# A row maximum on one core: 20 loads instead of 22, narrower parts for GpSimd, another ending

## The chip, the cores and the metric

The kernel runs on 1 core of one Trainium2 chip. The metric is the device time in microseconds (us) of one execution. Times are compared between fast runs only: one of the first runs of the kernel before took 183.46 us, over 1.5% above the others, counts as slow and is left out of every ratio.

## The reference

The input is 32 x 512 x 1024 float32 (67.1 MB), the output the maximum over the last axis (64 KB).

```python
def reference(x: np.ndarray) -> np.ndarray:      # x: (32, 512, 1024) float32
    return np.max(x, axis=-1).astype(np.float32)
```

The 16,384 rows of 1024 are 128 on each of the 128 partitions. In this text "row" means one row on each partition, 512 KiB.

## The kernel before

The loads go into a ring of 46 rows. Each is reduced by one instruction of the vector engine (DVE). Load sizes in rows, numbered from 0, get smaller so that little is left to do when the last has landed:

```python
BLOCKS = [
    [15, 15, 15, 13, 13, 11, 9, 9, 6, 6],
    [3, 3, 2, 1, 1, 1, 1, 1, 1, 1],
]
RING = 46
BY_GPSIMD = {8: 1, 9: 3, 12: 1}      # whole rows of these loads
MERGE = {9: 8, 15: 9, 18: 12}        # after which load DVE takes the result
```

Five whole rows go by another road: TensorE transposes eight parts of 128 x 128 into PSUM, the memory that it writes (`turn`), ScalarE copies them to SBUF, where the ring lies, GpSimd takes the maximum across partitions, TensorE transposes it back (`back`), and DVE merges the eight partial maxima of each row.

```python
    for c in range(C):                                   # turn; C is 8
        in_turn("PE", nc.tensor.transpose(out=ps[:, c * P:(c + 1) * P],
            in_=rows[:, k, c * P:(c + 1) * P], identity=ident))
    nc.scalar.copy(out=sb, in_=ps)
    nc.gpsimd.partition_all_reduce(top, sb, P, bass_isa.ReduceOp.max)
    # ... cut: back, the loop over the loads
```

The last row comes in two halves; the second reduce takes the first one's result along as an extra column. The first 112 columns of results are stored once the last whole-row load is reduced, the last 16 at the end, both from ScalarE's queue.

```python
    in_turn("DVE", nc.vector.reduce_max(out=tail[:, PAD - 1:PAD], in_=half, axis=X))
    in_turn("DVE", nc.vector.reduce_max(out=res[:, I - 1:], in_=tail[:, PAD - 1:], axis=X))
    store = nc.scalar.dma_start(out=views[0][0], in_=views[0][1])
    tc.add_manual_dep(store.ins, reduce.ins.name, SYNC, reason="behind the loads")
    nc.scalar.dma_start(out=views[1][0], in_=views[1][1])
```

## Time and profile before

| what | kernel before |
|---|---|
| median of the first three runs | 164.4 us |
| span of the profiled run | 162.6 us |
| DVE busy | 135.0 us, 83% |
| GpSimd (POOL) busy | 16.3 us, 10% |
| load queue, share of the 16 DMA engines' time | 96.6% |
| DVE waiting for loads | 24.3 us, of which 18.9 for the first |

A profile has several views. The page gives busy shares and groups of equal instructions. The timeline gives start, length and, in brackets, the idle time ahead of an instruction with what ended it. The chain is the sequence of work and waits that led to the end. One thing to know of the timeline: it brackets waits of some size only. Waits below about 0.15 us must be read from the distance between starts. The lines of before are in the prediction below.

The groups show what one instruction costs. The columns are line, engine, operation, shapes, count, then busy time and mean length in ns, then idle time ahead:

```profile
L139 DVE TENSOR_REDUCE res<-ring 128x1 f32<-128x1024 f32 x8 | 9.4, 1212 | 0.0
L106 POOL PARTITION_ALL_REDUCE top<-sb x5 | 16.1, 3255 | 138.8 <-ACT sb L104 138.8
L143 DVE TENSOR_REDUCE res<-fetched 128x1 f32<-128x8 f32 x2 | 0.3, 154 | 0.0
```

A row costs DVE 1.2 us by itself, a merge 0.15 us, and a row costs GpSimd 3.3 us.

### The profile page before, as it was taken

The page shows a single profiled execution, that of the slowest core. Times are in us where ns is not written, and L with a number is a line of the kernel's source. Part 1 is how long each engine was busy: PE and PEld are TensorE (multiplying, and loading weights), DVE is VectorE, ACT ScalarE, POOL GpSimd, SP SyncE. Part 2 cuts the span into 40 slices and gives each one's busy share as a digit, 9 for nine tenths or more (in the row PEclk, how much of TensorE's full clock was granted, in tenths as well). Part 3 has the DMA queues.
Part 4 walks back from the last instruction along what each step waited for, and adds up shares of the span by engine and source line. Part 5 has one row for each costly group of instructions (what it writes and reads, how often), then busy time and mean ns, then how long its engine had stood idle before and what let it go on. Part 6 is the DMA issues. An engine that isn't in the chain of part 4 may idle for free.

```text
span 162.6 us, 293 instructions
## 1 busy us (share of the span) xinstructions
PE 13.0 (8%) x80; PEld 11.7 (7%) x80; DVE 135.0 (83%) x33; ACT 6.3 (4%) x6; POOL 16.3 (10%) x9
## 2 busy tenths in 40 slices
PE   0000000000000000000000000000000040943520
PEld 0000000000000000000000000000000030933420
DVE  3000079995999779999996999999999999999994
ACT  3000000000000000000000000000000011240200
POOL 0000000000000000000000000000000007099910
PEclk9999999999999999999999999999999999985555
DMA  7999699988999799999998989999999999999990
GB/s 242 484 484 438 287 484 484 484 378 348 484 484 484 333 498 432 445 419 419 419 419 387 499 388 427 417 426 408 417 435 435 471 399 426 423 418 409 406 368 16
DMA packets 3456, 67.18 MB, mean 413 GB/s; under 512 B 640, under 2 KB 640, under 8 KB 1792
## 3 DMA queue, kind: packets, MB, share of 16 engines
q1 hardware_dynamic: 3168, 67.11, 96.6%
q10 hardware_dynamic: 288, 0.07, 0.2%
HBM read 67.11 MB, written 0.07 MB: 413 GB/s over the span
## 4 chain that ended last, share of the span: by engine, by line
DVE 54%; DMA 44%; SPq 0%; issue 0%
DVE res L139 53%; DMA ring<-in_x_dram 44%; DVE res L156 0%; DVE tail L155 0%; SPq L133 0%; DVE res L143 0%
## 5 line engine op out<-in xcount | busy, mean ns | idle before, releaser
L139 DVE TENSOR_REDUCE res<-ring 128x1 f32<-128x1024 f32 (+6 forms) x20 | 132.1, 6653 | 24.3 <-DMA ring<-in_x_dram 24.3
L106 POOL PARTITION_ALL_REDUCE top<-sb x5 | 16.1, 3255 | 138.8 <-ACT sb L104 138.8
L98 PE MATMUL ps<-ident,ring 128*128 128x128 f32 x40 | 8.1, 382 | 134.2 <-DMA ring<-in_x_dram 131.8
L98 PEld LDWEIGHTS ps<-ident,ring 128*128 128x128 f32 x40 | 7.1, 204 | 134.3 <-issue 134.2
L104 ACT COPY sb<-ps 128x1024 f32<-128x1024 f32 x5 | 5.1, 1013 | 144.9 <-PE ps L98 143.0
L115 PE MATMUL fetched<-ident,top 1*128 1x1 f32 x40 | 5.0, 243 | 9.1 <-POOL top L106 9.1
L115 PEld LDWEIGHTS fetched<-ident,top 1*128 1x128 f32 x40 | 4.6, 214 | 10.3 <-POOL top L106 9.8
L104 ACT ACT_TABLE_LOAD x1 | 1.3, 1283 | 0.7 <-PEq L176 0.7
L76 DVE MEMSET ident<- 128x128 f32 x1 | 0.2, 165 | 0.8 <-PEq L176 0.8
L156 DVE TENSOR_REDUCE res<-tail 128x1 f32<-128x513 f32 x1 | 0.7, 686 | 0.0
L155 DVE TENSOR_REDUCE tail<-ring 128x1 f32<-128x512 f32 x1 | 0.7, 675 | 0.0
L83 DVE TENSOR_SCALAR rowno<-rowno 32x1 f32<-32x1 f32 x3 | 0.4, 147 | 0.1
L143 DVE TENSOR_REDUCE res<-fetched 128x1 f32<-128x8 f32 (+1 forms) x3 | 0.5, 161 | 0.0
L78 DVE TENSOR_TENSOR_SCAN colno<-ident 128x128 f32<-128x128 f32 x1 | 0.4, 425 | 0.0
L85 DVE TENSOR_SCALAR ident<-colno,rowno 128x128 f32<-128x128 f32 x1 | 0.3, 287 | 0.0
L80 DVE STREAM_TRANSPOSE rowno<-colno 128x32 f32<-128x32 f32 x1 | 0.2, 211 | 0.0
L176 POOL MEMSET const-float32-0.0<- 128x1 f32 x1 | 0.1, 99 | 0.2 <-issue 0.2
L176 POOL MEMSET const-uint8-127<- 128x1 uint8 x1 | 0.1, 103 | 0.0
L176 POOL MEMSET const-bfloat16-1.0<- 128x1 bf16 x1 | 0.1, 102 | 0.0
L176 POOL MEMSET const-float32-1.0<- 128x1 f32 x1 | 0.1, 99 | 0.0
L77 DVE MEMSET rowno<- 128x32 f32 x1 | 0.1, 85 | 0.0
## 6 DMA issues: line engine op xcount, KB each, us to landing
ring<-in_x_dram SPq DMA_DIRECT2D x3, 7680.0 KB, 38.4
ring<-in_x_dram SPq DMA_DIRECT2D x2, 6656.0 KB, 34.6
ring<-in_x_dram SPq DMA_DIRECT2D x2, 4608.0 KB, 37.8
ring<-in_x_dram SPq DMA_DIRECT2D x2, 3072.0 KB, 31.9
ring<-in_x_dram SPq DMA_DIRECT2D x1, 5632.0 KB, 28.6
ring<-in_x_dram SPq DMA_DIRECT2D x7, 512.0 KB, 22.3
ring<-in_x_dram SPq DMA_DIRECT2D x2, 1536.0 KB, 34.9
ring<-in_x_dram SPq DMA_DIRECT2D x1, 1024.0 KB, 33.4
```

Of the source, the lines that this page charges most:

```text
L78: in_turn("DVE", nc.vector.tensor_tensor_scan(out=colno, data0=ident, data1=ident, initial=-1.0, op0=ALU.add, op1=ALU.mult))
L83: in_turn("DVE", nc.vector.tensor_scalar(out=part, in0=part, scalar1=float(q * 32), scalar2=None, op0=ALU.add))
L85: in_turn("DVE", nc.vector.tensor_scalar(out=ident, in0=colno, scalar1=rowno[:, 0:1], scalar2=None, op0=ALU.is_equal))
L98: in_turn("PE", nc.tensor.transpose(out=ps[:, c * P:(c + 1) * P], in_=rows[:, k, c * P:(c + 1) * P], identity=ident,))
L104: nc.scalar.copy(out=sb, in_=ps)
L106: nc.gpsimd.partition_all_reduce(top, sb, P, bass_isa.ReduceOp.max)
L115: in_turn("PE", nc.tensor.transpose(out=backs[j][:, k, c:c + 1], in_=tops[j, k][0:1, c * P:(c + 1) * P], identity=ident[0:1, 0:1],))
L139: reduce = in_turn("DVE", nc.vector.reduce_max(out=cols[:, :n - m], in_=xc[:, :n - m, :], axis=X))
L143: in_turn("DVE", nc.vector.reduce_max(out=tiles[i][1], in_=backs[i], axis=X))
L155: in_turn("DVE", nc.vector.reduce_max(out=tail[:, PAD - 1:PAD], in_=half, axis=X))
L156: in_turn("DVE", nc.vector.reduce_max(out=res[:, I - 1:], in_=tail[:, PAD - 1:], axis=X))
L176: nc = _bacc.Bacc("TRN2", target_bir_lowering=False, num_devices=1)
```

## The change

It aims at the last 70 us, where DVE runs without a break behind the loads: other load sizes, GpSimd's share cut into parts 128 wide and spread over five loads, the last two rows in three pieces, and the first store in three parts by partitions.

```diff
-    [15, 15, 15, 13, 13, 11, 9, 9, 6, 6],
-    [3, 3, 2, 1, 1, 1, 1, 1, 1, 1],
+    [15, 15, 15, 14, 12, 11, 9, 8, 7, 6],
+    [4, 3, 2, 2, 1, 1, 1],
-BY_GPSIMD = {8: 1, 9: 3, 12: 1}
-MERGE = {9: 8, 15: 9, 18: 12}
+SHARED = {7: (2, 3), 9: (4, 4), 11: (3, 3), 13: (2, 3), 16: (1, 1)}   # load: (rows, parts of each)
+MERGE = {8: (7,), 12: (9,), 15: (11,), 18: (13, 16)}
 ... (order of TensorE's work, loads issued up to three ahead: cut)
+    if m and parts < C:                    # the rest of shared rows, to PSUM
+        maximum(share(j)[:, parts, :], rows(j)[:, n - m:, parts * P:])
-    in_turn("DVE", nc.vector.reduce_max(out=tail[:, PAD - 1:PAD], in_=half, axis=X))
-    in_turn("DVE", nc.vector.reduce_max(out=res[:, I - 1:], in_=tail[:, PAD - 1:], axis=X))
+    nc.sync.dma_start(out=piece, in_=xb[:, S - 2, :D - K])                  # 689 columns
+    nc.sync.dma_start(out=res[:, AT:AT + K + W], in_=pair[:, D - K:D + W])  # 671
+    nc.sync.dma_start(out=res[:, MID:], in_=pair[:, D + W:])                # 688
+    latest_row = maximum(res[:, AT - 1:AT], piece)
 ... (one reduce for both halves of the pair, merges, the last reduce: cut)
-    store = nc.scalar.dma_start(out=views[0][0], in_=views[0][1])
+    for p, q in ((0, 48), (48, 96), (96, P)):
+        store = nc.scalar.dma_start(out=views[0][0][p:q], in_=views[0][1][p:q])
```

More of the change, by code (lines that the diff above doesn't have):

```diff
@@ L13 @@
 BLOCKS = [
-    [15, 15, 15, 13, 13, 11, 9, 9, 6, 6],
-    [3, 3, 2, 1, 1, 1, 1, 1, 1, 1],
+    [15, 15, 15, 14, 12, 11, 9, 8, 7, 6],
+    [4, 3, 2, 2, 1, 1, 1],
 ]
 RING = 46
-TENSOR = {
-    8: [("turn", 8, 0), ("back", 8, 0)],
-    9: [("turn", 9, 0), ("turn", 9, 1), ("turn", 9, 2), ("back", 9, 0)],
-    12: [("turn", 12, 0), ("back", 9, 1), ("back", 9, 2), ("back", 12, 0)],
-}
-BY_GPSIMD = {8: 1, 9: 3, 12: 1}
-MERGE = {9: 8, 15: 9, 18: 12}
+SHARED = {7: (2, 3), 9: (4, 4), 11: (3, 3), 13: (2, 3), 16: (1, 1)}
+TENSOR = [
+    ("turn", 7, 0), ("back", 7, 0), ("turn", 9, 0), ("turn", 9, 1),
+    ("back", 9, 0), ("turn", 11, 0), ("turn", 11, 1), ("back", 9, 1),
+    ("turn", 13, 0), ("back", 11, 0), ("back", 11, 1), ("turn", 16, 0),
+    ("back", 13, 0), ("back", 16, 0),
+]
+MERGE = {8: (7,), 12: (9,), 15: (11,), 18: (13, 16)}
 NOSYNC = mybir.DependencyInfo(mybir.DependencyClass.NoSync, mybir.DependencyReason.DATA)
@@ L53 @@
     allr = ctx.enter_context(tc.tile_pool(name="allr", bufs=2))
-    psum = ctx.enter_context(tc.tile_pool(name="psum", bufs=3, space=bass.MemoryType.PSUM))
-    psmall = ctx.enter_context(tc.tile_pool(name="psmall", bufs=2, space=bass.MemoryType.PSUM))
+    psum = ctx.enter_context(tc.tile_pool(name="psum", bufs=2, space=bass.MemoryType.PSUM))
+    psmall = ctx.enter_context(tc.tile_pool(name="psmall", bufs=4, space=bass.MemoryType.PSUM))
     ring = once.tile([P, RING, D], F32)
-    res = once.tile([P, I], F32)
-    PAD = 16
-    tail = once.tile([P, PAD + H], F32)
+    W = 336
+    K = W - 1
+    AT = I + 16
+    MID = AT + K + W + 17
+    res = once.tile([P, MID + D - W], F32)
     latest = {}
@@ L86 @@
         out=ident, in0=colno, scalar1=rowno[:, 0:1], scalar2=None, op0=ALU.is_equal))
-    tiles = {}
-    tops = {}
-    backs = {}
-    def turn(j, k):
-        rows, cols = tiles[j]
-        ps = psum.tile([P, D], F32)
-        for c in range(C):
-            in_turn("PE", nc.tensor.transpose(
-                out=ps[:, c * P:(c + 1) * P],
-                in_=rows[:, k, c * P:(c + 1) * P],
-                identity=ident,
-            ))
-        sb = turned.tile([P, D], F32)
-        nc.scalar.copy(out=sb, in_=ps)
-        top = allr.tile([P, D], F32)
-        nc.gpsimd.partition_all_reduce(top, sb, P, bass_isa.ReduceOp.max)
-        tops[j, k] = top
-    def back(j, k):
-        if j not in backs:
-            fetched = psmall.tile([P, BY_GPSIMD[j], C], F32)
-            backs[j] = fetched
-        for c in range(C):
-            in_turn("PE", nc.tensor.transpose(
-                out=backs[j][:, k, c:c + 1],
-                in_=tops[j, k][0:1, c * P:(c + 1) * P],
-                identity=ident[0:1, 0:1],
-            ))
-    at = first = j = 0
+    loads = []
+    first = at = 0
     views = []
-    for loads in BLOCKS:
-        S = sum(loads) + (loads is BLOCKS[-1])
+    for sizes in BLOCKS:
+        S = sum(sizes) + 2 * (sizes is BLOCKS[-1])
         xb = xf[first * P:(first + S) * P, :].rearrange("(p i) d -> p i d", p=P)
@@ L128 @@
         b = 0
-        for n in loads:
+        for n in sizes:
             if at + n > RING:
                 at = 0
-            xc = ring[:, at:at + n, :]
-            nc.sync.dma_start(out=xc, in_=xb[:, b:b + n, :])
-            cols = res[:, first + b:first + b + n]
-            m = BY_GPSIMD.get(j, 0)
-            tiles[j] = xc[:, n - m:, :], cols[:, n - m:]
-            for what, i, k in TENSOR.get(j, []):
-                (turn if what == "turn" else back)(i, k)
-            reduce = in_turn("DVE", nc.vector.reduce_max(
-                out=cols[:, :n - m], in_=xc[:, :n - m, :], axis=X))
-            if j in MERGE:
-                i = MERGE[j]
-                in_turn("DVE", nc.vector.reduce_max(out=tiles[i][1], in_=backs[i], axis=X))
+            loads.append((at, n, xb[:, b:b + n, :], first + b))
@@ L144, with chunks, rows, turn @@
             at += n
             b += n
-            j += 1
         first += S
     assert first == I
+    def chunks(j):
+        m, parts = SHARED[j]
+        per = max(1, C // parts)
+        return [(r, min(per, m - r)) for r in range(0, m, per)]
+    def rows(j):
+        start, n, _, _ = loads[j]
+        return ring[:, start:start + n, :]
+    tops = {}
+    backs = {}
+    def turn(j, c):
+        m, parts = SHARED[j]
+        r, q = chunks(j)[c]
+        W = q * parts * P
+        ps = psum.tile([P, D], F32)
+        for i in range(q):
+            for c0 in range(parts):
+                k = i * parts + c0
+                in_turn("PE", nc.tensor.transpose(
+                    out=ps[:, k * P:(k + 1) * P],
+                    in_=rows(j)[:, loads[j][1] - m + r + i, c0 * P:(c0 + 1) * P],
+                    identity=ident,
+                ))
+        sb = turned.tile([P, D], F32)
+        in_turn("ACT", nc.scalar.copy(out=sb[:, :W], in_=ps[:, :W]))
+        top = allr.tile([P, D], F32)
+        in_turn("POOL", nc.gpsimd.partition_all_reduce(
+            top[:, :W], sb[:, :W], P, bass_isa.ReduceOp.max))
+        tops[j, c] = top
@@ new lines, in share, with back @@
+    def share(j):
+        m, parts = SHARED[j]
+        if j not in backs:
+            fetched = psmall.tile([P, parts + (parts < C), m], F32)
+            backs[j] = fetched
+        return backs[j]
+    def back(j, c):
+        m, parts = SHARED[j]
+        r, q = chunks(j)[c]
+        for i in range(q):
+            for c0 in range(parts):
+                k = i * parts + c0
+                in_turn("PE", nc.tensor.transpose(
+                    out=share(j)[:, c0, r + i:r + i + 1],
+                    in_=tops[j, c][0:1, k * P:(k + 1) * P],
+                    identity=ident[0:1, 0:1],
+                ))
@@ new lines, in maximum, with merge @@
+    def maximum(out, in_):
+        return in_turn("DVE", nc.vector.reduce_max(out=out, in_=in_, axis=X))
+    def merge(j):
+        for i in MERGE.get(j, ()):
+            _, k, _, c0 = loads[i]
+            q, _ = SHARED[i]
+            maximum(res[:, c0 + k - q:c0 + k], share(i).rearrange("p k m -> p m k"))
+    issued = done = 0
+    todo = list(TENSOR)
+    for j in range(len(loads)):
+        while issued < len(loads) and issued < j + 3:
+            start, n, src, _ = loads[issued]
+            held = any(s < start + n and start < s + k for s, k, _, _ in loads[j:issued])
+            if held:
+                break
+            nc.sync.dma_start(out=rows(issued), in_=src)
+            issued += 1
+        while todo and todo[0][1] < (j if todo[0][0] == "back" else issued):
+            what, i, c = todo.pop(0)
+            (turn if what == "turn" else back)(i, c)
+        _, n, _, col = loads[j]
+        m, parts = SHARED.get(j, (0, 0))
+        if n > m:
+            maximum(res[:, col:col + n - m], rows(j)[:, :n - m, :])
+        if m and parts < C:
+            maximum(share(j)[:, parts, :], rows(j)[:, n - m:, parts * P:])
+        merge(j)
@@ L150 @@
+    for what, i, c in todo:
+        assert what == "back"
+        back(i, c)
     if at + 1 > RING:
         at = 0
-    half = ring[:, at, :H]
-    nc.sync.dma_start(out=half, in_=xb[:, b, :H])
-    nc.sync.dma_start(out=tail[:, PAD:], in_=xb[:, b, H:])
-    in_turn("DVE", nc.vector.reduce_max(out=tail[:, PAD - 1:PAD], in_=half, axis=X))
-    in_turn("DVE", nc.vector.reduce_max(out=res[:, I - 1:], in_=tail[:, PAD - 1:], axis=X))
-    store = nc.scalar.dma_start(out=views[0][0], in_=views[0][1])
@@ L160 @@
-    tc.add_manual_dep(store.ins, reduce.ins.name, SYNC, reason="behind the loads")
+    piece = ring[:, at, :D - K]
+    nc.sync.dma_start(out=piece, in_=xb[:, S - 2, :D - K])
+    pair = xb[:, S - 2:, :].rearrange("p i d -> p (i d)")
+    nc.sync.dma_start(out=res[:, AT:AT + K + W], in_=pair[:, D - K:D + W])
+    nc.sync.dma_start(out=res[:, MID:], in_=pair[:, D + W:])
+    latest_row = maximum(res[:, AT - 1:AT], piece)
+    merge(len(loads))
+    maximum(
+        bass.AP(tensor=res.tensor, offset=res.offset + I - 2,
+                ap=[list(res.ap[0]), [MID - 1 - (I - 2), 2]]),
+        res[:, AT - 1:AT + K + W].rearrange("p (r k) -> p r k", r=2))
@@ L161 @@
+    merge(len(loads) + 1)
+    maximum(res[:, I - 1:I], res[:, MID - 1:])
+    for p, q in ((0, 48), (48, 96), (96, P)):
+        store = nc.scalar.dma_start(out=views[0][0][p:q], in_=views[0][1][p:q])
+        tc.add_manual_dep(store.ins, latest_row.ins.name, SYNC, reason="behind the loads")
     nc.scalar.dma_start(out=views[1][0], in_=views[1][1])
```

## The prediction

> **What bounds the kernel now.** I read the page first: busy shares, then the chain that ended last, then the groups by shape, then the timeline of the vector engine (DVE) and of the load queue (SPq). The page's first lines:
>
> ```profile
> span 162.6 us, 293 instructions
> PE 13.0 (8%) x80; PEld 11.7 (7%) x80; DVE 135.0 (83%) x33; ACT 6.3 (4%) x6; POOL 16.3 (10%) x9
> q1 hardware_dynamic: 3168, 67.11, 96.6%
> DVE 54%; DMA 44%; SPq 0%; issue 0%
> ```
>
> Loads keep the DMA engines busy for 96.6% of the span and DVE is busy for 83%, so the two are nearly balanced. The chain shows how they share the path. In order of time (start, length, what):
>
> ```profile
> 1.15 38.43 DMA ring<-in_x_dram
> ...
> 39.60 16.16 DVE res L139
> ...
> 55.78 33.41 DMA ring<-in_x_dram
> ...
> 89.22 53.79 DVE res L139 x6
> ...
> 159.05 0.60 DVE tail L155
> ...
> 159.67 0.69 DVE res L156
> ```
>
> Until 89.22 us the chain passes through transfers; from there it is DVE without a break, to 160.36. So what counts is how long DVE waits before it becomes the bound, and how much work it has after that. The waits stand in the timeline (start, busy, then in brackets the idle time before):
>
> ```profile
> 39.60 16.15 DVE L139 TENSOR_REDUCE res<-ring 128x15 f32<-128x15360 f32 x1 [1.99 <-DMA ring<-in_x_dram]
> 57.75 30.08 DVE L139 TENSOR_REDUCE res<-ring 128x15 f32<-128x15360 f32 x2 [1.99 <-DMA ring<-in_x_dram]
> 89.22 53.79 DVE L139 TENSOR_REDUCE res<-ring 128x13 f32<-128x13312 f32 x6 [1.40 <-DMA ring<-in_x_dram]
> ```
>
> A start after a wait is also the time at which a load landed. More landings are to be had from the load queue: it has at most 8 loads in flight, so late loads issue when the one 8 places before has landed. The queue's timeline has issues at
>
> ```profile
> 131.68 0.33 SPq L133 DMA_DIRECT2D ring<-in_x_dram  x1
> 138.98 0.33 SPq L133 DMA_DIRECT2D ring<-in_x_dram  x1
> 146.35 0.33 SPq L133 DMA_DIRECT2D ring<-in_x_dram  x1
> 150.13 0.33 SPq L154 DMA_DIRECT2D tail<-in_x_dram  x1
> ```
>
> and the last (the tail) lands 9.0 us after issue by the page's table of DMA issues, at 159.13.
>
> **A model of the loads.** Below, "row" is one row of 1024 per partition, 512 KiB. A load of n rows takes a*n + c of a saturated queue. The third load of 15 rows lands 57.75 - 39.60 = 18.15 us after the second, so 15a + c = 18.15. From 57.73 to the tail at 159.13 there are 83 rows in 19 loads: 83a + 19c = 101.40. This gives a = 1.2047 us a row, c = 0.074 us a load. Check: load 8, counting from 0, has 61 rows and 6 loads after 57.73, so 131.66; the queue shows 131.68.
>
> **What the Trainium skill says.** "DMA: Bandwidth & Descriptors", section Bandwidth, puts the fabric ceiling at 435 GB/s. Here 524,288 bytes in 1.2047 us are 435 GB/s: it agrees, the queue has nothing to give but c. The section Rules for kernel authors of the same page says of two transfers to disjoint partition halves not to bother, as both use all 16 engines; no run yet shows this for a store. "VectorE: DVE Perf Modes", the perf-mode tier table, gives tensor_reduce only the 1x mode. It agrees: one row is 1024/0.96 GHz = 1.067 us, and the group of 1-row reduces has a mean of 1212 ns, the 15-row one 16153 ns, both columns/0.96 plus 0.15. The section on the TRN2 errata there says that a fixed part is exposed between instructions. Here back-to-back reduces start columns/0.96 plus 0.065 to 0.09 us apart (53.71 us from 89.22 to the first merge for 51,200 columns in 6 reduces; 11.13 us for 10,240 in the next 6). I use 0.08. No page gives the width dependence of the GpSimd all-reduce.
>
> **The change, part by part.** The loads change from 15,15,15,13,13,11,9,9,6,6 and 3,3,2,1x7,.5,.5 to 15,15,15,14,12,11,9,8,7,6 and 4,3,2,2,1,1,1 and three pieces of two thirds of a row.
>
> *Idle time of DVE.* Load 3 now lands at 57.73 + 14a + c = 74.67. DVE is done with load 2 at 57.75 + 16.15 = 73.90, and starts 0.03 after landing, at 74.70: a wait of 0.80. Load 4 lands at 89.20 as before, and DVE finishes load 3 at 74.70 + 14.93 + 0.07 = 89.70, so the wait of 1.40 is gone. **Saving: 0.60 us.**
>
> *Work of DVE.* GpSimd had 1 + 3 + 1 whole rows, 40 parts of 128 columns. It gets 2x3 + 4x4 + 3x3 + 2x3 + 1x1 = 38. So it takes less, not more; DVE gets 256 columns, **0.27 us**. After load 2, DVE has 24 instructions from load 3 on against 22 before (the order of instructions shows five added reduces of the rest of shared rows, which write to PSUM, and one more merge; there are fewer load reduces): 2 x 0.08 = **0.16 us**. Net: -0.60 + 0.27 + 0.16 = **-0.17 us**.
>
> The same as a sum: from 74.70, 69 whole rows (70,656 columns), the rests of shared rows (1280 + 2048 + 1920 + 1280 + 896 = 7,424), merges (52) and the pieces (689 + 672 + 689) are 80,182 columns, 83.52 us; 23 gaps of 0.08 are 1.84, and the end of the last one 0.15. DVE ends at 160.21, against 160.36. The same sum for before, 66,601 columns from 89.22, gives 69.38 + 21 x 0.08 + 0.15 = 160.43, so it is good to 0.1.
>
> *Does DVE wait again?* I put the landings beside the DVE starts, load by load. Nowhere does a wait come out, but slack is thin: load 5 lands 102.53 and DVE is ready at 102.56; load 8 131.66 against 131.90; load 10 143.86 against 143.96; load 13 152.51 against 152.70; the last piece 158.98 against 159.36. The sizes look chosen so that both reach the end together. Two loads fewer save the queue 0.15 us (159.13 to 158.98), which only counts if DVE waits.
>
> *GpSimd's side chain.* The last merges (loads 13 and 16) come up on DVE at 159.17 and 159.27. The all-reduce takes 3.23 us for 1024 columns; in proportion (an estimate) 2.4 for 768, 1.2 for 384 and 0.4 for 128. Load 13 lands 152.51; six transposes 1.5, copy 0.8 (1.01 at 1024), semaphores 0.2: 155.0; all-reduce to 157.4. Load 16 lands 156.35, its all-reduce queues behind and ends at 157.9; the seven transposes back bring the last result to about 158.7. That is 0.5 us ahead of need, off the path.
>
> *Stores.* Before, the first-block store issued at 159.08, 0.38 us long, the last at 160.39 after the last reduce, and the span ended 2.29 us after DVE did. Now three stores wait for the first piece's reduce (about 158.4) and their three issues end by 159.6, before the last reduce. 48 and 32 partitions are multiples of 16, so (by the skill's page on DMA, section on why a semaphore grows by 16) each still uses all engines. Cost on the path: 0. The 2.29 stays.
>
> Span: 160.2 + 2.29 = 162.5. The measured time was 164.43 for a span of 162.6, so add 1.8: 164.3; with the 0.17 saving taken from 164.4 instead, 164.2. I choose 164.2.
>
> **Rivals.** *The all-reduce has a large fixed part.* There were five calls of one width, so the profile can't separate fixed from proportional; seven calls of mixed width would pay it more often. If the fixed part is f, the chain of loads 13 and 16 ends about 1.1f later: f = 0.5 is absorbed, f = 1 delays the end by 0.6 us (164.8), a wholly fixed 3.2 us by 3 us (167). For: seven narrow calls are a risk and a custom instruction must be started up. Against: 1024 columns take 3.15 ns each, which looks like per-column work, and someone cut parts narrow on purpose.
>
> *Late loads: DVE waits for transfers again.* With slacks of 0.03 to 0.3 us, a queue that is 0.3 late (a piece that does not start at an even address, stores beside the last piece) puts up to 0.3 us back: 164.4 to 164.5. For: the slacks. Against: the model meets the checked landing within 0.02, and the stores move data only 0.9 us after issue, when the last piece is already through.
>
> *The transfers are the floor.* Even a free DVE cannot end before the last piece: 158.98 + 0.03 + 0.87 for its reduce, 159.88. So the gain is limited to about 0.5 us, 163.9. The reverse, reduces into PSUM dearer than mine, costs 5 x 0.05 = 0.25 us and wipes the gain out: 164.4.
>
> **Range and chances.** All but the first rival stay within 163.9 to 164.6; the first has a tail upwards. Fast runs before agree to 0.03 us. I take 163.8 to 164.9. 2% is 3.3 us: faster by that is ruled out by the floor, slower needs an all-reduce that does not shrink with width or something not seen: faster 0.005, same 0.975, slower 0.02.
>
> **What would show it.** DVE idle before load 3 of 0.8 us and none after; DVE work of 135.4 us in all; last reduce starting near 159.4 and ending 160.2; the last piece landing near 159.0; all-reduces of 2.4 and 0.4 us at 768 and 128 columns; merges without a wait on PE. A wait of DVE on the last merges would show the first rival, one on a transfer the second. I am wrong if the time leaves the range, above all if the all-reduces of 128 columns take over 1 us.

## The result

The changed kernel took 164.07 us (median of 6 runs, 163.96 to 164.16), the kernel before 164.37 us. The ratio is 0.9984, with a 95% interval of 0.9971 to 0.9998. A ratio is the mean time of one kernel's fast runs over that of the other's of the same rounds, so it is not quite the ratio of the quoted medians. The predicted time was 164.2, the range 163.8 to 164.9: right, and "same" at a limit of 2%, with a gain of 0.3 us.

First lines of the page of the changed kernel, as shown of before in the prediction:

```profile
span 162.3 us, 305 instructions
PE 14.0 (9%) x76; PEld 12.0 (7%) x76; DVE 135.4 (83%) x35; ACT 6.3 (4%) x8; POOL 16.2 (10%) x11
q1 hardware_dynamic: 2880, 67.11, 96.7%
DVE 57%; DMA 36%; issue 5%; DVEq 0%
```

DVE is busy 0.4 us longer than before (135.4 against 135.0), and the span is 0.3 us shorter. So the gain is in waiting, not in work. (0.6 us less of waiting and 0.4 us more of work do not make 0.3: waits too short for a bracket are in neither figure.) The same part of the DVE timeline as before:

```profile
57.70 16.16 DVE L168 TENSOR_REDUCE res<-ring 128x15 f32<-128x15360 f32 x1 [1.99 <-DMA ring<-in_x_dram]
74.64 55.86 DVE L168 TENSOR_REDUCE res<-ring 128x14 f32<-128x14336 f32 x5 [0.79 <-DMA ring<-in_x_dram]
```

The wait before load 3 is 0.79 us, and the one of 1.40 us before load 4 is gone. In all DVE waits 23.7 us for loads. Now the end, DVE and ScalarE's store queue (ACTq), with GpSimd's last two all-reduces and the transposes back (PE L161):

```profile
155.10 3.19 POOL L143 PARTITION_ALL_REDUCE top<-sb  x2 [1.06 <-ACT sb L141]
...
157.65 0.95 PE L161 MATMUL fetched<-ident,top 1*128 1x1 f32 x7 [0.76 <-POOL top L143]
158.23 1.33 ACTq L221 DMA_DIRECT2D out_dram<-res  x3
...
159.01 0.22 DVE L168 TENSOR_REDUCE res<-fetched 128x2 f32<-128x8 f32 x2
159.15 0.86 DVE L168 TENSOR_REDUCE res<-res 128x1 f32<-128x689 f32 x1
160.04 0.36 ACTq L223 DMA_DIRECT2D out_dram<-res  x1
```

Three things are to be seen. The last results of GpSimd are back in PSUM at 158.60 (157.65 + 0.95), 0.4 us ahead of the merges at 159.01. The three short stores hold ScalarE's queue for 1.33 us, until 159.56, and the last store issues right after DVE at 160.04. DVE ends at 160.01 (159.15 + 0.86), against 160.36 before.

As the first loads land up to 0.3 us earlier or later from run to run, I compare kernels below by the **DVE length**: from the start of DVE's third reduce to the end of its last. It is 160.36 - 57.75 = 102.61 us before and 160.01 - 57.70 = 102.31 after. It comes from one profile of each kernel and has noise of its own: the two kernels with the old ending below, whose DVE work is the same, differ by 0.08, and in two profiles (sizes alone, whole rows) loads landed 0.16 to 0.19 us later than in the others, counted from the third reduce, for no known reason. A difference under about 0.2 us in one profile is therefore not shown by it alone.

### The profile page after: what moved, and what is told of

Read it like the earlier page. It is cut to its first block, busy times and chain, and to the rows that moved or that the text cites. A ratio compares the mean times of both kernels' runs of the same rounds, so it can differ in the third digit from the quotient of the medians.

```text
span 162.3 us, 305 instructions
## 1 busy us (share of the span) xinstructions
PE 14.0 (9%) x76; PEld 12.0 (7%) x76; DVE 135.4 (83%) x35; ACT 6.3 (4%) x8; POOL 16.2 (10%) x11
## 4 chain that ended last, share of the span: by engine, by line
DVE 57%; DMA 36%; issue 5%; DVEq 0%
DVE res L168 52%; DMA ring<-in_x_dram 36%; DVE fetched L168 5%; DVEq L249 0%
## 5 line engine op out<-in xcount | busy, mean ns | idle before, releaser
L168 DVE TENSOR_REDUCE res<-ring 128x15 f32<-128x15360 f32 (+10 forms) x15 | 124.1, 8302 | 23.7 <-DMA ring<-in_x_dram 23.7
L135 PE MATMUL ps<-ident,ring 128*128 128x128 f32 x38 | 9.3, 425 | 133.8 <-DMA ring<-in_x_dram 133.8
L141 ACT COPY sb<-ps 128x768 f32<-128x768 f32 (+3 forms) x7 | 5.1, 739 | 150.2 <-PE ps L135 150.2
L168 DVE TENSOR_REDUCE fetched<-ring 128x2 f32<-128x1280 f32 (+3 forms) x5 | 8.5, 1699 | 0.0
L161 PE MATMUL fetched<-ident,top 1*128 1x1 f32 x38 | 4.8, 243 | 10.8 <-DVE fetched L168 7.3
L161 PEld LDWEIGHTS fetched<-ident,top 1*128 1x128 f32 x38 | 4.5, 213 | 12.5 <-issue 8.0
L168 DVE TENSOR_REDUCE res<-res 128x2 f32<-128x672 f32 (+1 forms) x2 | 1.7, 858 | 0.0
L168 DVE TENSOR_REDUCE res<-fetched 128x2 f32<-128x8 f32 (+3 forms) x5 | 0.7, 158 | 0.0
```

Source lines behind the costliest of these rows:

```text
L135: in_turn("PE", nc.tensor.transpose(out=ps[:, k * P:(k + 1) * P], in_=rows(j)[:, loads[j][1] - m + r + i, c0 * P:(c0 + 1) * P], identity=i ...
L141: in_turn("ACT", nc.scalar.copy(out=sb[:, :W], in_=ps[:, :W]))
L161: in_turn("PE", nc.tensor.transpose(out=share(j)[:, c0, r + i:r + i + 1], in_=tops[j, c][0:1, k * P:(k + 1) * P], identity=ident[0:1, 0:1],))
L168: return in_turn("DVE", nc.vector.reduce_max(out=out, in_=in_, axis=X))
```

## The experiments

Two theories stood behind the twelve runs. **DVE alone** (how the chain of waits reads at first sight): after the last long wait only DVE's work counts. **Balance**: the landings of the loads (the times at which their data are complete in the ring) stand so close ahead of DVE's reduces that time saved on DVE returns as waits, and each part of the change is worth something only beside the others. All runs gave correct results.

### The load sizes alone, in the kernel before

```diff
-    [15, 15, 15, 13, 13, 11, 9, 9, 6, 6],
+    [15, 15, 15, 14, 12, 11, 9, 9, 6, 6],
```

> The kernel before with one edit: loads 3 and 4 of 14 and 12 rows instead of 13 and 13. Theory A, the step of the prediction taken literally (the changed sizes take 0.60 us of waiting off DVE): DVE idle for transfers falls from 24.3 to 23.7 us, DVE ends 0.5 to 0.6 us earlier (bounded by the tail's landing at 159.1 plus 0.7), time near 163.85 us, ratio to before 0.997. Theory B, balance: DVE arrives earlier at the later loads, which have not landed, and waits there (by the landing model 0.4 us at load 7 and 0.3 us at load 11, counted from 0, and the rest in bits near the end); DVE idle adds up to the same, DVE ends at 160.3 to 160.4, ratio 1.000.

Measured: 164.31 us against 164.31, ratio 0.9998 (0.9985 to 1.0010). Nothing is gained. The timeline of DVE shows where the 0.6 us went:

```profile
124.19 18.41 DVE L139 TENSOR_REDUCE res<-ring 128x9 f32<-128x9216 f32 x3 [0.30 <-DMA ring<-in_x_dram]
...
146.33 7.86 DVE L139 TENSOR_REDUCE res<-ring 128x3 f32<-128x3072 f32 x5 [0.34 <-DMA ring<-in_x_dram]
```

These waits, at loads 7 and 11, do not exist in the kernel before, and DVE's waiting for loads is 24.2 us in all, against 24.3. Balance holds. In this one profile the DVE length was 102.77 us, 0.16 more than before, as the loads from load 10 on came 0.16 to 0.18 us later; why is open, and the times don't show it.

### The old sizes in the changed kernel

```diff
-    [15, 15, 15, 14, 12, 11, 9, 8, 7, 6],
+    [15, 15, 15, 13, 13, 11, 9, 8, 7, 6],
```

> The changed kernel with loads 3 and 4 of 13 and 13 rows again. A and B both expect the wait of 1.4 us before load 4 back and load 3's wait gone, but differ from the run above in size: in the new sizes behind it B's landing model finds DVE late by 0.5 us at the end (160.5 us against 160.0), time 164.55, ratio to before 1.001. A: plus 0.6 us, 164.65. If the swap costs nothing here, as B expects for the kernel before, the sizes 14 and 12 do not matter in either and the gain came from the ending.

Measured: 164.44 us, ratio 1.0007 (0.9993 to 1.0021), DVE length 102.75, which is 0.44 more than the changed kernel's. So the same swap that is worth nothing in the kernel before is worth about 0.4 us in the changed one, whose later sizes and shares have room for it. It was expected at 0.5. The intervals of the two ratios just overlap; the timeline carries this reading: DVE reaches load 10 at 86.71 us from the third reduce, against 86.13, and no landing holds it after load 4.

### GpSimd takes more, or less, of load 7

```diff
-SHARED = {7: (2, 3), ...
+SHARED = {7: (2, 4), ...      # the other run: (2, 2)
```

> The changed kernel with GpSimd taking four instead of three parts of each of the two rows of load 7: DVE has 256 columns, 0.27 us, less to do. If DVE alone bounds from 74.6 us on (the chain of waits read literally), DVE ends 0.27 us earlier, near 159.75, time 163.8. If transfers hold it just as tightly (B), the saved time turns into waits at loads 8, 10 and on, DVE ends at 160.0, time 164.07 as the changed kernel.

> The changed kernel with GpSimd taking two instead of three parts of each row of load 7, 256 columns or 0.27 us more for DVE. The opposite of the run that gave it less and gained nothing: DVE has 0.1 us of waits left to absorb it in, so by the model it ends 0.18 us later, time 164.25. If it is bound by transfers alone: no change. If by DVE alone: plus 0.27, 164.35.

Measured: with four parts 164.08 us, ratio 0.9984, DVE length 102.31, the changed kernel's to the hundredth. With two parts 164.11 us, ratio 0.9987, DVE length 102.41. Taking 0.27 us off DVE gains nothing; adding 0.27 us costs 0.10 in the length, less than the 0.18 that I expected and too little to be shown by one profile, and nothing clear in the times. The first case can be followed in the timeline of the kernel with four parts:

```profile
130.32 1.22 DVE L168 TENSOR_REDUCE fetched<-ring 128x2 f32<-128x1024 f32 x1
131.54 7.62 DVE L168 TENSOR_REDUCE res<-ring 128x7 f32<-128x7168 f32 x1
...
139.15 2.27 DVE L168 TENSOR_REDUCE res<-ring 128x2 f32<-128x2048 f32 x1
...
143.74 4.42 DVE L168 TENSOR_REDUCE res<-ring 128x4 f32<-128x4096 f32 x1
```

```profile
143.73 0.33 SPq L206 DMA_DIRECT2D res<-in_x_dram  x1
```

The second fence is the load queue: by the prediction's reading, this issue, 8 places behind load 10, marks that load 10 has landed. The changed kernel has 139.41 and 143.83 for the last two starts, 4.42 us apart; here they are 4.59 apart with the same work between. DVE came early, load 10 was not there until 143.73, and DVE started 0.01 us after it. From the third reduce on, the start at load 10 is at 86.14 us in this kernel and at 86.13 in the changed one: the saved time is gone by then. "DVE alone" has fallen.

### One load in three transfers

```diff
-            nc.sync.dma_start(out=rows(issued), in_=src)
+            k = 3 if issued == 6 else n
+            for r in range(0, n, k):
+                nc.sync.dma_start(out=rows(issued)[:, r:r + k, :], in_=src[:, r:r + k, :])
```

> The changed kernel with the transfer of load 6 (9 rows) issued as three of 3 rows, DVE's reduces unchanged. At load 6 itself DVE has 0.9 us of slack. By the landing model, two more transfers put all later landings 0.15 us back. If DVE alone bounds there: no change, 164.07. If landings hold DVE as tightly (B): DVE waits 0.15 us at load 10 and ends at 160.15, time 164.2.

Measured: 164.32 us, ratio to before 0.9998 (0.9985 to 1.0010), DVE length 102.47, 0.16 more than the changed kernel. DVE's work is the same to 0.1 us (135.4), and at load 6 it had slack. All five times (164.29 to 164.46) lie above those of the changed kernel (163.96 to 164.16), though the intervals of the two ratios overlap. The queue shows where the time goes:

```profile
144.07 0.33 SPq L208 DMA_DIRECT2D res<-in_x_dram  x1
```

This is load 10's landing, 86.30 us after the third reduce, against 86.12 in the changed kernel, and DVE starts on it at 144.08. So two more transfers go with a landing 0.18 us later. The prediction's model says 0.15 (2 x 0.074) and agrees, but this is not a confirmation: the whole-row run below, with no transfer added, has load 10 at 86.31 too, and seven others with the changed sizes up to load 10 have it at 86.12 to 86.20.

### The first store in one piece

```diff
-    for p, q in ((0, 48), (48, 96), (96, P)):
+    for p, q in ((0, P),):
```

> The changed kernel with the first block's store in one piece. The store is not on the path in either: span and time of the changed kernel within 0.1 us (162.3 span, 164.07). A rival, that three short issues let the last store through sooner: the last store would issue or land later by the difference, 0.2 us or more after DVE's end than the 2.3 us of the changed kernel.

Measured: 164.24 us (164.00 to 164.28), ratio 0.9990 (0.9978 to 1.0003), DVE length 102.33. The last store issues 0.03 us after DVE ends and takes 1.4 us to landing in both kernels. The median is 0.17 us above the changed kernel's, but the load start of this profile is 0.07 us later too, and the intervals of the two overlap. No effect of the split is seen.

### The ending of before in the changed kernel, with three stores and with one

```diff
-    [4, 3, 2, 2, 1, 1, 1],          # then two rows in pieces of 689, 671, 688 columns
+    [4, 3, 2, 2, 1, 1, 1, 1],       # then one row in two halves
```

> The changed kernel with the ending of before: one more load of one row, then the last row in two halves, in place of two rows in three pieces. By the landing model and DVE's gaps DVE ends at 160.25 against 160.0: time 164.3, so that without the new ending most of the gain is gone. If the ending doesn't matter, 164.07. The number of DVE reduces is the same in both, so a difference comes from the lag of DVE behind the landings, not from DVE work.

Measured: 165.07 us, ratio 1.0040 (1.0027 to 1.0052). My 164.3 was a miss by 0.8 us. The timeline shows that DVE is not the reason:

```profile
159.55 1.32 ACTq L213 DMA_DIRECT2D out_dram<-res  x3
159.55 0.69 DVE L168 TENSOR_REDUCE res<-res 128x1 f32<-128x513 f32 x1
160.96 0.38 ACTq L215 DMA_DIRECT2D out_dram<-res  x1
```

DVE ends at 160.24. The last store issues 0.72 us later, at 160.96: it stands in ScalarE's queue behind three stores that started late, as with this ending the reduce that releases them comes 0.7 us before DVE's end, not 1.8. The second run tests this, with the same ending and one store:

> The changed kernel with the old ending, as in the run before, but the first block's store in one piece. In that run DVE ended at 160.24, 0.37 us later relative to the third load's landing than in the changed kernel, yet the last store issued only at 160.96: three short stores that start at 159.55 kept ScalarE's queue until then. If so, the last store now issues 0.1 us after DVE's end, near 160.3, the time falls by 0.7 us to 164.35 to 164.45. If the cause is elsewhere, the last store stays near 160.9 and the time at 165.1.

Measured: 164.49 us, ratio 1.0007 (0.9993 to 1.0020), and the end is

```profile
159.62 0.69 DVE L168 TENSOR_REDUCE res<-res 128x1 f32<-128x513 f32 x1
160.34 0.34 ACTq L215 DMA_DIRECT2D out_dram<-res  x1
```

The store issues 0.03 us after DVE. So splitting the store is worth nothing beside the new ending (run above) and costs 0.5 to 0.6 us in this run (0.5 when each time is set against before in its own rounds).

One thing differs from the kernel before: its first store waits for the last whole-row reduce; the stores here wait for the reduce of the first half, which comes later. Had the three been released as before, at 158.79 (the whole-row reduce starts at 157.57 and takes 1.22), they would have left the queue by about 158.79 + 0.03 + 1.32 = 160.14, ahead of DVE's end at 160.24. This is an estimate that no run tests; by it the cost belongs to three stores together with their late release, not to the old ending as such.

The ending itself costs 0.29 us of DVE length here (102.60) and 0.37 with three stores (102.68), where the model said 0.25.

### The new ending alone, in the kernel before

```diff
-    [3, 3, 2, 1, 1, 1, 1, 1, 1, 1],     # then the last row in halves
+    [3, 3, 2, 1, 1, 1, 1, 1, 1],        # then two rows in pieces of 689, 671, 688; one store
```

> The kernel before with the new ending alone: its last two rows in three pieces, one store. By the landing model DVE ends 0.06 us earlier, the last landing is the same: time 164.3, ratio 0.9995. If the ending alone brought the gain of 0.3 us, ratio 0.998. With the swap of 13, 13 for 14, 12 alone, which gave 0, this tells whether any single part carries the gain.

Measured: 164.42 us against 164.32, ratio 1.0003 (0.9990 to 1.0015), DVE length 102.66 (before 102.61). The ending alone gains nothing either. So neither the sizes nor the ending gains anything alone, and taking either out of the changed kernel loses about the whole 0.3 us (164.44, and 164.49 with one store).

### GpSimd's share: the last row wider, whole rows, none

```diff
-SHARED = {..., 16: (1, 1)}
+SHARED = {..., 16: (1, 4)}                                # run 1
+SHARED = {7: (1, 8), 9: (2, 8), 11: (1, 8), 13: (1, 8)}   # run 2, order of TensorE's work to match
+SHARED = {}                                               # run 3
```

> The changed kernel with GpSimd taking four parts of the very last whole row (load 16) instead of one. DVE has 384 columns, 0.40 us, less; GpSimd's last all-reduce is 512 wide (1.8 us by 0.34 us plus 2.8 ns a column, fitted to the changed kernel's trace) instead of 128 (0.69). If only DVE work counts: DVE ends at 159.6 to 159.9, bounded by the last landing. If GpSimd's chain (the prediction's first rival) has little slack: the last result comes back near 160.6, DVE waits 1.7 us on TensorE for the merge and ends near 161.6, time 165.7.

> The changed kernel with GpSimd taking whole rows as before: 1, 2, 1 and 1 rows of loads 7, 9, 11 and 13 (40 parts instead of 38, fewer DVE instructions). If parts of 128 are only a way to fill in work: DVE ends near 159.9, time 164.0. By the model of the side chain the last all-reduce, 3.2 us and started after load 13, comes back near 160.05, DVE waits 1 us for it and ends near 161.0: time 165.1.

> The changed kernel without GpSimd's share: DVE has 38 parts of 128 columns, 5.07 us, more, and ten reduces into and out of PSUM less one, about 0.7 us, less. By the model DVE ends 4.4 us later, at 164.4, time 168.5. All of it must come after load 7, while the landings stay.

Measured: 165.87 us (ratio 1.0089), 165.03 us (1.0041) and 168.52 us (1.0253), against the expected 165.7, 165.1 and 168.5. The verdict on the first two is one line of each timeline, the merge of GpSimd's last result. First the kernel with the wider last row, then that with whole rows:

```profile
160.70 0.16 DVE L168 TENSOR_REDUCE res<-fetched 128x1 f32<-128x5 f32 x1 [1.62 <-PE fetched L161]
```

```profile
160.22 0.17 DVE L167 TENSOR_REDUCE res<-fetched 128x1 f32<-128x8 f32 x1 [0.84 <-PE fetched L160]
```

By columns DVE has 0.4 us less to do in the first (3 parts of 128) and as many busy us (135.4) in the second, yet stands idle for 1.62 and 0.84 us on TensorE, which waits for GpSimd. This is the wait by which the prediction's first rival was to show itself. Here wide parts bring it about, not a large fixed part; the changed kernel stays 0.4 us clear of it with one part 128 wide of the last row and narrow parts of load 13. Without GpSimd, DVE has 4.5 us more to do on balance, and all of it is on the path (DVE length 106.85).

## Why the prediction was right

*The model of the loads* was right. It put load 3's wait at 0.80 us, measured 0.79, and the last landing at 158.98; the last piece issued at 147.52 and took 11.5 us by the table of issues, 159.0.

*The idle time of DVE* fell by the 0.60 us that the prediction had (24.3 to 23.7). What the prediction did not see is that this step is not the property of the sizes 14 and 12 by which it was worked out. Alone they give nothing (0.9998), and the waits turn up at loads 7 and 11. The working was saved by the check of every load for new waits, which took all sizes and shares of the changed kernel together.

*The work of DVE* was predicted at 135.4 us and measured at 135.4.

*The end of DVE* was predicted at 160.21 and measured at 160.01. This was mis-sized: the saving came out as 0.35 us in this pair of profiles (160.36 to 160.01) and 0.30 in the times, not 0.17. The term is the sum of the gaps between instructions. From 74.64 to 160.01 are 85.37 us; less 83.52 for columns and 0.15 for the last end, 1.70 us are left for 23 gaps, 0.074 each and not 0.08: 0.14 us. Another 0.06 us is that the loads started earlier in that profile. The gap itself is smaller still. In the runs with 13 and 13 rows and with two parts of load 7, where DVE is later, the same count leaves 1.47 us for 22 gaps and 1.52 for 23, 0.067 and 0.066 each. So of the 1.70 about 0.17 us are waits too short for a bracket. One is at load 16: its first reduce starts 0.14 us after the merge before it (156.20 to 156.34), in the run with two parts 0.08 (156.41 to 156.49). The prediction's "nowhere does a wait come out" was thus not quite right, and these waits fit that 0.27 us more of work put DVE's end back by 0.10 only.

Two slips in the prediction's sums change nothing that follows. Its check on the kernel before counts 21 gaps, but 21 instructions have 20; put right, it gives 160.35 against the measured 160.36. And the merges have 50 columns, not 52 (0.002 us).

*GpSimd's side chain* was predicted to end at 158.7 and ended at 158.60. The proportional widths were a little low: 2.50 us for 768 columns (2.4 expected) and 0.78 for 128 (0.4 expected). With 3.22 for 1024 this makes about 2.8 ns a column and a fixed part of 0.3 to 0.4 us, an amount that the prediction said would be absorbed.

*The stores* were off the path as predicted, but by 0.48 us only (159.56 to 160.04). That each still uses all engines fits the packets of their queue, 320 against 288 before, 16 for each added store. The run with the old ending shows that this was luck of the order rather than a property of stores.

*The second rival*, loads that come late, is the one to which the experiments give most weight: its slacks of 0.03 to 0.3 us are why nothing taken off DVE at load 7 helps, and they fit the loss of about 0.2 us with two more transfers.

What stays open: the narrow parts were not tried alone in the kernel before, whose sizes and shares do not fit them; the order of TensorE's work, the number of PSUM buffers and the loads issued ahead were not tried alone either; and the whole-row run is one placement of whole rows among many. No run beat the changed kernel; those with four and with two parts of load 7 and with one store equal it within the noise.

## What to carry to other kernels

Where loads and a compute engine are both nearly full (here 97% and 83% busy) and meet at the end, list for every load when it lands and when the engine is ready for it; a saving counts only if no later load turns it into a wait. Judge a change of sizes, of shares and of the ending together, since here sizes and ending were worth nothing when tried alone and the whole was worth 0.3 us. Leave the last issue of a queue clear of any short issues ahead of it, and measure their queue time, not only their bytes.

## What the Trainium skill lacked or had wrong

- "GPSIMD Engine Reference" has no cost by width for the all-reduce across partitions. Here: 0.78 us for 128 columns, 2.50 for 768, 3.22 for 1024.
- "DMA: Bandwidth & Descriptors", section Issuing engines are not separate DMA queues, calls the sequencer's time to start a DMA usually small beside the DMA itself. Three stores of 14 to 21 KB held ScalarE's queue for 1.32 us, 0.44 each, and put the last store 0.72 us behind DVE; with one store the time was 164.49 instead of 165.07 us (164.32 and 164.40 before, in their own rounds).
- The same page's section Rules for kernel authors advises against splitting a transfer by partitions, for bandwidth. The runs agree (no gain seen beside the new ending), and add that it can cost 0.5 to 0.6 us, where the stores are released only 0.7 us before the last result.
- No page gives the cost of one more transfer on a queue that is full anyway. Here it is 0.074 us, fitted; with two more, DVE's end came 0.16 us later in one profile, a shift that noise can make too.
